# A decoder layer in fp32r pieces: when sets are summed, how far down's operands are prepared, and where the last norms stand

## The chip, the cores and the metric

The kernel runs on one core of one Trainium2 chip. A core has five engines that run their own instruction streams in order: PE (TensorE, matmuls; PEld are its weight loads), DVE (VectorE), ACT (ScalarE), POOL (GpSimd) and SP (SyncE, which only issues transfers here). ACT and POOL can issue transfers too. An instruction waits on semaphores for what it needs; whatever stands behind it on its engine waits with it. The metric is the time of one execution in microseconds (us), as the median of several runs.

## The reference: what is computed

One layer over 1024 tokens of width 1024: an adaLN modulation from a conditioning vector, a mixer of two attentions with gates, a layer norm, a SwiGLU feed-forward and a second layer norm. The change touches the last two:

```python
def swiglu(u, w_gate_up, w_down):
    h = jnp.einsum('btd,df->btf', u, w_gate_up)
    hg, hu = jnp.split(h, 2, axis=-1)
    return jnp.einsum('btf,fd->btd', jax.nn.silu(hg) * hu, w_down)
...
    y = swiglu(u, w_gate_up[l], w_down[l])
    x = layer_norm(DEEPNORM_ALPHA * x + (1.0 + gate_f) * y, ln2_g[l], ln2_b[l])
```

The feed-forward width is 2816, which is 22 tiles of 128 rows.

## The kernel before, in words

**Numbers in two pieces.** A float32 operand is split: ACT copies it, rounded, to a high piece and DVE subtracts that from the original for the low piece (`split`, lines 169 and 170; for gate/up weights lines 144 and 145). A product is then three matmuls: high by high, high by low, low by high.

**Seven products for eight.** Both feed-forward matrices are multiplied by a Strassen-like scheme: sums and differences of the four quarters of each operand give seven products of half size in place of eight. Somebody has to make these sums.

**Gate/up** (the loop from line 1597) runs over 22 pairs p of a gate and an up tile, and for each over seven slots i, one product of 12 matmuls each. The split for a product is issued before the product two places earlier, and `w_hi`/`w_lo` have four buffers, so DVE works at most some three slots ahead of TensorE. POOL makes the sums of the weights (`Pairs.add`: steps 0 to 2 in slots 2 to 4 for the next pair, step 3 in slot 3 of the pair itself) and one sum of results in slot 4 (line 1639). In slot 6 of pairs 3 to 10 it also applies the first norm's gain and bias to a row block (`gain`, lines 1372 and 1373). SP loads the raw weights of pair p+2 in slot 4 (`gu.load`, line 112) and stores the pair's h tile (line 1644).

**Sets for down** (`sum_set`, line 1520). Down needs sums of its operands: 11 sets "w" of `w_down` rows and 11 sets "h" of pairs of h tiles. A set loads two tiles as four halves on ACT's queue, waits five calls, makes two operations on DVE, in the next call two more, and two calls later stores four halves on SP's queue (line 1545). `sums_ahead` is called once in each slot, and in down once per unit, and steps up to three lanes, each with its own buffers, from pairs 4, 8 and 11 on; only lane 1 may begin a set in down. An h set may begin as soon as its second tile's pair is over.

**Down** has seven products in the order 0, 1, 2, 3, 5, 4, 6, each of 11 units u. A unit is one raw pair of tiles of 128x512 (`dn_load`, two SP transfers of 256 KB, four raw buffers), one split of 128x1024 on ACT and DVE into one of 14 operand places (`dn_prepare`: 8 in the pool `bigu`, 6 in `low`), and 12 matmuls: 3 for each of four banks t. Unit u's step first issues the splits up to unit u + 11, with loads four units beyond. After a product, four `dn_add` (lines 1671 and 1672: gate times PSUM, added to the row block) and, where a row half is final, `half_stats` (line 1268) stand on DVE. Products five and seven go on in banks that the products before them in those banks have filled and `dn_add` has read: the fifth in those of the fourth, the seventh in those of the sixth.

**The second norm.** `norm_shared` (line 1290) makes a row block's moments (DVE, with one square root on ACT), normalizes it on ACT (line 1296), and returns `finish`: times gain on DVE (line 1299), plus bias on POOL (line 1300), out on SP. In the sixth product steps j = 1, 3, 5, 7 begin the norms of rows 0 to 3 and the steps behind them finish these. In the seventh product the bank loop is outside, so that a bank is done after 33 matmuls; its row's adds, statistics and norm follow, and the last row uses `norm_quick` (lines 1283 and 1286).

Everything is under a manual schedule: an engine's order is the order of the calls.

Of the kernel before, what the change touches and what calls it, by code (L numbers as in the profile page):

```python
# [11 lines left out]
F32R = mybir.dt.float32r  # L12
I32 = mybir.dt.int32
AF = mybir.ActivationFunctionType
OP = mybir.AluOpType
# [3 lines left out]
P = 128  # L19
# [130 lines left out]
def decoder_layer(ctx: ExitStack, tc: tile.TileContext, I, out, dbg=None):  # L150
# [1139 lines left out]
    def norm_shared(tb, gb, dst):  # L1290

        z = zrow(tb)
        mv, rs = moments(tb)
        nc.vector.reciprocal(rs[:, 0:1], rs[:, 0:1])
        nc.vector.scalar_tensor_tensor(rs[:, 1:2], mv[:, 0:1], -1.0, rs[:, 0:1], op0=OP.mult, op1=OP.mult)
        nc.scalar.activation(z, z, AF.Identity, bias=rs[:, 1:2], scale=rs[:, 0:1])

        def finish():
            nc.vector.tensor_tensor(z, z, gb[:, 0], op=OP.mult)  # L1299
            nc.gpsimd.tensor_tensor(z, z, gb[:, 1], op=OP.add)  # L1300
            nc.sync.dma_start(dst[tb * P:(tb + 1) * P], z)

        return finish
# [214 lines left out]
    sets = [(kind, j) for kind in "wh" for j in range(NP)]  # L1518

    def sum_set(kind, j, x, y):  # L1520
        for i, halves in enumerate((x, y)):
            f = 2 * j + i
            src = I["w_down"][f * P:(f + 1) * P, :] if kind == "w" else h_d[f]
            for t in range(2):
                nc.scalar.dma_start(halves[t], src[:, t * TH:(t + 1) * TH])
        for _ in range(5):
            yield
        (x0, x1), (y0, y1) = x, y
        tt = nc.vector.tensor_tensor
        if kind == "w":  # L1530
            tt(x0, x1, x0, op=OP.subtract)
            tt(x1, y1, x1, op=OP.subtract)
            yield
            tt(y1, y1, x0, op=OP.subtract)
            tt(y0, y0, y1, op=OP.subtract)
        else:
            tt(y1, x1, y1, op=OP.add)
            tt(x1, x0, x1, op=OP.subtract)
            yield
            tt(x0, y1, x0, op=OP.subtract)  # L1540
            tt(y0, y0, x0, op=OP.subtract)
        yield
        yield
        for i, tile in enumerate((x0, x1, y0, y1)):
            nc.sync.dma_start((wt2_d if kind == "w" else hs_d)[j, i], tile)
        for _ in range(4):
            yield

    lanes = [None] * 3

    def lane_tiles(lane):
        if lane == 0:
# [8 lines left out]
        return [[x[:, H0], x[:, H1]] for x in tiles]  # L1561

    def sums_ahead(p, i):
        for lane, first in enumerate((4, 8, 11)):
            if lanes[lane] and next(lanes[lane], "end") == "end":
                lanes[lane] = None
            if (not lanes[lane] and (p, i) > (first, 0) and p < (20, NF + 1, 20)[lane] and sets
                    and (sets[0][0] == "w" or 2 * sets[0][1] + 1 < p)):
                lanes[lane] = sum_set(*sets.pop(0), *lane_tiles(lane))
                next(lanes[lane])  # L1570

# [3 lines left out]
    def dn_load(upto):  # L1575
        while len(dn_raw) < min(upto, DN):
# [8 lines left out]
            nc.sync.dma_start(raw[:, 1], {0: I["w_down"][rows, H0], 1: I["w_down"][rows, H0], 2: wt2_d[j, 3], 3: wt2_d[j, 0],  # L1585
                                          4: wt2_d[j, 1], 5: I["w_down"][rows, H1], 6: wt2_d[j, 2]}[i])

    def dn_prepare(upto, ahead):
        while len(dn_op) < min(upto, DN):
            u = len(dn_op)  # L1590
            dn_load(u + 1)
            dn_op[u] = pools["bigu" if u % 14 < 8 else "low"].tile([P, 2, 2, TH], F32R, name="dn", tag="big")
            split(dn_op[u][:, 0], dn_op[u][:, 1], dn_raw[u])
            dn_load(u + 1 + ahead)

    n = 0
    for p in range(NF):
# [11 lines left out]
        for i in range(7):  # L1609
# [35 lines left out]
            if (p, i) == (0, 4):  # L1645
                nc.scalar.activation(g[0], g[0], AF.Silu)
            if p + 1 < NF:
                if i == 4 and p + 2 < NF:
                    gu.load(p + 2)
                if i in (2, 3, 4) and p:  # L1650
                    gu.add(p + 1, i - 2)
# [22 lines left out]
    def dn_mac(ps, u, t, first, last):  # L1674
        op, c = dn_op[u], slice(t * P, (t + 1) * P)
        for n, (x, y) in enumerate(((0, 0), (0, 1), (1, 0))):
            nc.tensor.matmul(ps, op[:, x, 0, c], op[:, y, 1], start=first and n == 0, stop=last and n == 2,  # L1677
                             skip_group_check=True)

    st8 = gx.tile([P, TH], F32, name="s3", bufs=1)  # L1680
# [4 lines left out]
    for n, i in enumerate(ORDER[:-1]):  # L1685
        if i in (1, 3):
            bank = [(ps_f, ps_x)[t // 2].tile([P, TH], F32, name=("pf", "px")[t // 2]) for t in range(4)]
        ps = bank if i % 2 else bank_a
        for j in range(NP):
            u = n * NP + j  # L1690
            dn_prepare(u + 12, 4)
            for t in range(4):
                dn_mac(ps[t], u, t, i in (0, 1, 3) and j == 0, j == NP - 1)
            sums_ahead(NF, 1)
            if i == 4:
                if 1 <= j < 9 and j % 2:
                    ends.append(norm_shared(j // 2, gb2, out))
                elif 1 <= j < 9:
                    ends.pop(0)()
        tb0, eh, first = {0: (0, 0, True), 1: (0, 0, False), 2: (0, 1, True), 3: (4, 1, True), 4: (4, 1, False),  # L1700
                          5: (0, 1, False)}[i]
        for t in range(4):
            dn_add(tb0 + t, eh, ps[t], first)
            if not first:
                half_stats(tb0 + t, eh)
    dn_prepare(DN, 4)
    for t in range(4):
        for j in range(NP):
            dn_mac(bank_a[t], 6 * NP + j, t, False, j == NP - 1)
        dn_add(4 + t, 0, bank_a[t], True)  # L1710
        half_stats(4 + t, 0)
        while ends:
            ends.pop(0)()
        if t == 3:
            norm_quick(7, gb2, out)
        else:
# [78 lines left out]
```

## Time and profile before

| what | value |
|---|---|
| median of 3 runs | 1812.08 us (1809.89 to 1812.53) |
| the profiled execution's own time | 1811.52 us |
| its span, first to last instruction | 1809.7 us |
| mean granted TensorE clock | 0.993 |
| busy: PE, DVE, ACT, POOL | 1766.1, 1218.5, 844.0, 570.1 us |
| gate/up pairs 4 to 21 | about 1209 to 1572 us |
| down | about 1572 to 1798 us |

How to read it: a row of a timeline gives start and duration in us, engine, line of the kernel, operation, tile written <- tiles read, and in brackets how long the engine had been idle and what ended that. A row of waits gives who waited for whom, the total, the times and the longest. In a window, each engine has its busy time and in brackets its count of instructions. PE's matmuls overlap in the records, so that their pitch, not their duration, tells their cost. `dn` stands for the down raws and operands alike, `zt` for the row blocks, `pf` and `px` for PSUM banks, `wt_d` in a down load for the w sets.

### The profile page before, as it was taken

Reading aid. Unit: us, or ns where it says so; the run is one execution under the profiler, and the core shown is the slowest. Engines: PE = TensorE matmul, PEld = TensorE weight load, DVE = VectorE, ACT = ScalarE, POOL = GpSimd, SP = SyncE. Lnnn points to the kernel's source line nnn. Section 1 sums busy time; section 2 is a strip of 40 time slices with the busy share of each in tenths; the row PEclk is TensorE's granted clock in tenths of the full one; section 3 lists DMA queues with packets and bytes.
Section 4 is the critical chain, followed back from the end, with each engine's and each line's share of the span. In section 5 each row is a group of like instructions: output and inputs, shape, how many; then the busy total and the mean of one; then the engine's idle time right before and its main releaser. Section 6 shows DMA issues by size and latency. Waiting matters only on the chain.

```text
span 1809.7 us, 24697 instructions
## 1 busy us (share of the span) xinstructions
PE 1766.1 (98%) x8774; PEld 1446.2 (80%) x8774; DVE 1218.5 (67%) x2094; ACT 844.0 (47%) x1731; POOL 570.1 (32%) x357
## 2 busy tenths in 40 slices
PE   9999999999999999999999999999999999999977
PEld 7888888888888888888888888887777778888865
DVE  7655566566656766568648855778786775668576
ACT  6544544444445677765542225743333333444431
POOL 0232233233233332135205734166663333200021
PEclk9999999999999999999999999999999999999998
DMA  9222333333332332266577341155457675596731
GB/s 361 85 71 82 99 84 93 101 84 105 89 83 82 90 94 71 83 233 241 178 232 249 135 151 54 60 189 183 174 188 266 233 279 199 175 316 226 231 121 58
DMA packets 131099, 277.29 MB, mean 153 GB/s; under 512 B 19296, under 2 KB 29088, under 8 KB 130976
## 3 DMA queue, kind: packets, MB, share of 16 engines
q1 hardware_dynamic: 116544, 246.80, 41.2%
q10 hardware_dynamic: 13968, 27.33, 4.4%
q8 instruction: 69, 1.13, 0.3%
q0 software_dynamic: 464, 1.58, 0.2%
q14 instruction: 54, 0.44, 0.1%
HBM read 203.99 MB, written 58.03 MB: 145 GB/s over the span
## 4 chain that ended last, share of the span: by engine, by line
PE 85%; DVE 8%; issue 3%; ACT 2%; DMA 1%; POOL 1%; ACTq 0%; DVEq 0%; SPq 0%; POOLq 0%
PE pf L1037 16%; PE pj L191 9%; PE pj L193 9%; PE pj L192 9%; PE pf L1677 7%; PE p L1037 6%; PE s L623 4%; PE p L191 3%; PE p L193 3%; PE p L192 3%; PE po L684 3%; PE pt L661 3%; PE px L1677 2%; DVE w_lo L145 1%; PE pf L191 1%
## 5 line engine op out<-in xcount | busy, mean ns | idle before, releaser
L191 PE MATMUL pj<-u,w_hi 128*128 128x512 f32 x736 | 302.5, 411 | 0.0
L193 PE MATMUL pj<-u,w_lo 128*128 128x512 f32 x736 | 288.7, 392 | 0.0
L192 PE MATMUL pj<-u,w_hi 128*128 128x512 f32 x736 | 288.1, 391 | 0.0
L550 POOL TENSOR_TENSOR rb<-rb,sin_t 128x512 f32<-128x512 f32 x64 | 85.6, 1338 | 518.6 <-DVE rb L548 449.3
L145 DVE TENSOR_TENSOR w_lo<-r,w_hi 128x512 fp32r<-128x512 f32 x128 | 135.2, 1065 | 85.9 <-ACT w_hi L144 82.1
L1677 PE MATMUL pf<-dn 128*128 128x512 f32 x726 | 172.3, 392 | 13.4 <-DVE g L1671 13.4
L79 DVE TENSOR_TENSOR w_lo<-w_raw,w_hi 128x512 fp32r<-128x512 f32 x132 | 124.2, 944 | 81.4 <-ACT w_hi L78 80.8
L1677 PEld LDWEIGHTS pf<-dn 128*128 128x128 f32 x726 | 137.6, 190 | 42.6 <-issue 13.8
L191 PEld LDWEIGHTS pj<-u,w_hi 128*128 128x128 f32 x736 | 138.5, 188 | 31.7 <-issue 5.8
L193 PEld LDWEIGHTS pj<-u,w_lo 128*128 128x128 f32 x736 | 138.2, 188 | 30.8
L639 ACT ACTIVATE probs<-probs,st 128x128 f32<-128x128 f32 (+1 forms) x320 | 145.6, 461 | 30.9 <-DVE st L628 30.5
L192 PEld LDWEIGHTS pj<-u,w_hi 128*128 128x128 f32 x736 | 138.7, 188 | 22.4
L170 DVE TENSOR_TENSOR dn<-dn 128x1024 fp32r<-128x1024 f32 x77 | 94.9, 1251 | 50.5 <-ACT dn L169 49.6
L78 ACT ACTIVATE w_hi<-w_raw 128x512 fp32r<-128x512 f32 x132 | 81.8, 622 | 92.3 <-PE p L192 55.0
L169 ACT ACTIVATE dn<-dn 128x1024 fp32r<-128x1024 f32 x77 | 80.7, 1058 | 81.5 <-DMA dn<-wt_d 30.7
L551 POOL TENSOR_TENSOR r<-ra,rb 128x512 f32<-128x512 f32 x63 | 116.2, 1845 | 4.9
L663 ACT ACTIVATE ptsb<-pt 128x512 f32<-128x512 f32 (+1 forms) x128 | 63.5, 548 | 101.4 <-PE pt L661 101.1
L144 ACT ACTIVATE w_hi<-r 128x512 fp32r<-128x512 f32 x128 | 79.5, 623 | 32.4 <-DMA h_d<-g 6.3
L1300 POOL TENSOR_TENSOR zt<-zt,gb 128x1024 f32<-128x1024 f32 x7 | 20.3, 2895 | 214.6 <-DVE zt L1299 214.6
L564 ACT ACTIVATE qs<-r 64x1024 fp32r<-64x1024 f32 x38 | 40.2, 1058 | 100.7 <-POOL r L551 100.2
L565 DVE TENSOR_TENSOR qs<-r,qs 64x1024 fp32r<-64x1024 f32 x38 | 46.4, 1220 | 57.2 <-ACT qs L564 56.5
L126 POOL TENSOR_TENSOR s<-r 128x512 f32<-128x512 f32 x27 | 36.5, 1353 | 152.8 <-DVE w_lo L145 115.0
(417 smaller groups left out, 4362.8 us busy)
## 6 DMA issues: line engine op xcount, KB each, us to landing
w_raw<-in_w_in SPq DMA_DIRECT2D x100, 256.0 KB
r<-in_w_gate_up SPq DMA_DIRECT2D x44, 512.0 KB
a_raw<-in_w_ada SPq DMA_DIRECT2D x24, 512.0 KB
dn<-hs_d SPq DMA_DIRECT2D x44, 256.0 KB
dn<-wt_d SPq DMA_DIRECT2D x44, 256.0 KB
h_d<-g SPq DMA_DIRECT2D x39, 256.0 KB
dn<-h_d SPq DMA_DIRECT2D x33, 256.0 KB
dn<-in_w_down SPq DMA_DIRECT2D x33, 256.0 KB
```

Source lines behind the costliest of these rows:

```text
L78: self.nc.scalar.activation(hi, raw, AF.Copy)
L79: self.nc.vector.tensor_tensor(lo, raw, hi, op=OP.subtract)
L145: self.nc.vector.tensor_tensor(lo, src, hi, op=OP.subtract)
L170: nc.vector.tensor_tensor(lo, src, hi, op=OP.subtract)
L191: nc.tensor.matmul(ps, w[0], m[0], start=first, stop=False)
L192: nc.tensor.matmul(ps, w[0], m[1], start=False, stop=False)
L193: nc.tensor.matmul(ps, w[1], m[0], start=False, stop=last)
L550: eng.tensor_tensor(b, b, sin_t[:, s], op=OP.mult)
L551: eng.tensor_tensor(residue_half(res, r, t), by_residue(a, r), by_residue(b, r), op=OP.add)
L639: nc.scalar.activation(pr, pr, AF.Exp, scale=-1.0, bias=st[:, 0, h, b:b + 1], accum_out=st[:, 1, h, b:b + 1])
L1037: nc.tensor.matmul(ps, w[:, c], m[:, k], start=first and k == 0 and n == 0, stop=k == 3 and n == 2, skip_group_check=True)
L1677: nc.tensor.matmul(ps, op[:, x, 0, c], op[:, y, 1], start=first and n == 0, stop=last and n == 2, skip_group_check=True)
```

## The change

- `finish` adds the bias on DVE, not on POOL.
- A set's two pairs of DVE operations each wait for a granted slot: slots 0, 1, 5 and 6 of a pair, and every unit in down; a slot is granted to one lane only. A set stays in its lane one call longer after its stores. An h set that would begin in slots 0 to 2 waits for slot 3 where its tile belongs to the pair just before. The last h set is loaded on POOL's queue.
- `gu.load(p + 2)` is issued in slot 5, not 4.
- Down has 16 operand places, and 17 from unit 33 on: the weights' `w_hi`/`w_lo` buffers make two (such a unit is split in two halves), the `a_raw`/`a_lo` buffers one. Unit u's step issues splits up to unit u + 11 for u below 3, u + 13 up to 21 and u + 14 from 22 on; behind each product's last step the splits are brought up to 14 units beyond its end, ahead of its adds.
- The sixth product runs its last three units bank by bank, and the adds and statistics of a bank follow its matmuls.
- The norms of rows 0 and 1 begin in steps 3 and 5 of the sixth product; those of rows 2 and 3 in the seventh, at unit 5 of banks 0 and 1. There a bank's pending `finish` calls come ahead of its adds.

```diff
@@ norm_shared
         def finish():
             nc.vector.tensor_tensor(z, z, gb[:, 0], op=OP.mult)
-            nc.gpsimd.tensor_tensor(z, z, gb[:, 1], op=OP.add)
+            nc.vector.tensor_tensor(z, z, gb[:, 1], op=OP.add)
@@ sum_set
+        queue = nc.gpsimd if (kind, j) == ("h", NP - 1) else nc.scalar
...
-                nc.scalar.dma_start(halves[t], src[:, t * TH:(t + 1) * TH])
+                queue.dma_start(halves[t], src[:, t * TH:(t + 1) * TH])
         for _ in range(5):
             yield
...
+        while not granted():
+            yield
         if kind == "w":
             tt(x0, x1, x0, op=OP.subtract)
             tt(x1, y1, x1, op=OP.subtract)
             yield
+            while not granted():
+                yield
...
-        for _ in range(4):
+        for _ in range(5):
             yield
...
+    lanes, slot = [None] * 3, [False]
+
+    def granted():
+        free, slot[0] = slot[0], False
+        return free
@@ sums_ahead
+        slot[0] = p == NF or i in (0, 1, 5, 6)
...
-                    and (sets[0][0] == "w" or 2 * sets[0][1] + 1 < p)):
+                    and (sets[0][0] == "w" or 2 * sets[0][1] + 1 < p - (p < NF and i < 3))):
@@
+    places = ["bigu"] * 8 + ["low"] * 6 + ["w"] * 2
+
+    def dn_place(u):
+        if u == 33:
+            places.insert(0, "a")
+        place = places.pop(0)
+        places.append(place)
+        if place == "w":
+            hi, lo = [[wpool.tile([P, 512], F32R, name=s, tag=s, bufs=4) for _ in range(2)] for s in ("w_hi", "w_lo")]
+            for i in range(2):
+                split(hi[i], lo[i], dn_raw[u][:, i])
+            return hi, lo
+        if place == "a":
+            hl = [ev.tile([P, 2, TH], F32R, name=n, tag=n, bufs=1) for n in ("a_raw", "a_lo")]
+        else:
+            op = pools[place].tile([P, 2, 2, TH], F32R, name="dn", tag="big")
+            hl = [op[:, x] for x in range(2)]
+        split(*hl, dn_raw[u])
+        return [[x[:, i] for i in range(2)] for x in hl]
...
-            dn_op[u] = pools["bigu" if u % 14 < 8 else "low"].tile([P, 2, 2, TH], F32R, name="dn", tag="big")
-            split(dn_op[u][:, 0], dn_op[u][:, 1], dn_raw[u])
+            dn_op[u] = dn_place(u)
@@ gate/up loop
-                if i == 4 and p + 2 < NF:
+                if i == 5 and p + 2 < NF:
                     gu.load(p + 2)
@@ down
-        for j in range(NP):
+        shared = NP - 3 if i == 4 else NP
+        for j in range(shared):
             u = n * NP + j
-            dn_prepare(u + 12, 4)
+            dn_prepare(u + (12 if u < 3 else 14 if u < 22 else 15), 4)
...
-            if i == 4:
-                if 1 <= j < 9 and j % 2:
-                    ends.append(norm_shared(j // 2, gb2, out))
-                elif 1 <= j < 9:
-                    ends.pop(0)()
+            if i == 4 and j in (3, 5):
+                ends.append(norm_shared(j // 2 - 1, gb2, out))
+            elif ends:
+                ends.pop(0)()
+        dn_prepare(n * NP + NP + 14, 4)
         for t in range(4):
+            for j in range(shared, NP):
+                dn_mac(ps[t], n * NP + j, t, False, j == NP - 1)
             dn_add(tb0 + t, eh, ps[t], first)
             if not first:
                 half_stats(tb0 + t, eh)
-    dn_prepare(DN, 4)
     for t in range(4):
         for j in range(NP):
             dn_mac(bank_a[t], 6 * NP + j, t, False, j == NP - 1)
+            if t < 2 and j == 5:
+                ends.append(norm_shared(2 + t, gb2, out))
+        while ends:
+            ends.pop(0)()
         dn_add(4 + t, 0, bank_a[t], True)
         half_stats(4 + t, 0)
-        while ends:
-            ends.pop(0)()
```

More of the change, by code (lines that the diff above doesn't have):

```diff
@@ L1539, in sum_set @@
             yield
+            while not granted():
+                yield
             tt(x0, y1, x0, op=OP.subtract)
@@ L1545, in sum_set @@
             nc.sync.dma_start((wt2_d if kind == "w" else hs_d)[j, i], tile)
-        for _ in range(4):
+        for _ in range(5):
             yield
-    lanes = [None] * 3
+    lanes, slot = [None] * 3, [False]
+    def granted():
+        free, slot[0] = slot[0], False
+        return free
     def lane_tiles(lane):
@@ L1676, in dn_mac @@
         for n, (x, y) in enumerate(((0, 0), (0, 1), (1, 0))):
-            nc.tensor.matmul(ps, op[:, x, 0, c], op[:, y, 1], start=first and n == 0, stop=last and n == 2,
+            nc.tensor.matmul(ps, op[x][0][:, c], op[y][1], start=first and n == 0, stop=last and n == 2,
                              skip_group_check=True)
@@ L1688, in decoder_layer @@
         ps = bank if i % 2 else bank_a
-        for j in range(NP):
+        tb0, eh, first = {0: (0, 0, True), 1: (0, 0, False), 2: (0, 1, True), 3: (4, 1, True), 4: (4, 1, False),
+                          5: (0, 1, False)}[i]
+        shared = NP - 3 if i == 4 else NP
+        for j in range(shared):
             u = n * NP + j
-            dn_prepare(u + 12, 4)
+            dn_prepare(u + (12 if u < 3 else 14 if u < 22 else 15), 4)
             for t in range(4):
@@ L1694, in decoder_layer @@
             sums_ahead(NF, 1)
-            if i == 4:
-                if 1 <= j < 9 and j % 2:
-                    ends.append(norm_shared(j // 2, gb2, out))
-                elif 1 <= j < 9:
-                    ends.pop(0)()
-        tb0, eh, first = {0: (0, 0, True), 1: (0, 0, False), 2: (0, 1, True), 3: (4, 1, True), 4: (4, 1, False),
-                          5: (0, 1, False)}[i]
+            if i == 4 and j in (3, 5):
[3 more added lines that the diff above has]
+        dn_prepare(n * NP + NP + 14, 4)
         for t in range(4):
+            for j in range(shared, NP):
+                dn_mac(ps[t], n * NP + j, t, False, j == NP - 1)
             dn_add(tb0 + t, eh, ps[t], first)
```

## The prediction

> **What bounds the kernel now.** I read the page first, then the windows by stage, TensorE's waits, and the timelines at the places where TensorE stood still. The page's first row, and windows whose columns are length, then busy time and count of PE, PEld, DVE, ACT, POOL, then granted clock, DMA share, GB/s:
>
> ```profile
> PE 1766.1 (98%) x8774; PEld 1446.2 (80%) x8774; DVE 1218.5 (67%) x2094; ACT 844.0 (47%) x1731; POOL 570.1 (32%) x357
> ...
> 1209.00:1372.00 163.00, 156.32 (x679) 126.37 (x678) 124.19 (x124) 60.94 (x107) 100.88 (x56) 1.00 0.55 192
> 1372.00:1572.00 200.00, 195.02 (x841) 157.65 (x840) 136.56 (x170) 75.33 (x131) 68.92 (x47) 0.99 0.64 223
> 1753.00:1766.00 13.00, 0.00 (x0) 0.00 (x0) 10.35 (x11) 4.28 (x5) 6.51 (x2) 0.64 0.27 105
> 1766.00:1771.00 5.00, 4.79 (x13) 3.81 (x14) 4.79 (x9) 0.00 (x0) 0.00 (x0) 0.57 0.10 41
> ```
>
> TensorE sets the time, so a gain is only what it loses. Its pitch where nothing waits, and its largest wait, from the chain and the waits of the down stage:
>
> ```profile
> 1603.60 1.36 PE px L1677 x6
> ...
> ACT dn L169 <- DMA dn<-wt_d: 30.7, 23, 6.9
> PE pf L1677 <- DVE g L1671: 13.4, 1, 13.4
> ```
>
> Six matmuls in 1.36 us are 0.2267 us each. By that pitch the window 1209 to 1372 (pairs 4 to 11 of gate/up) holds 679 x 0.2267 = 153.9 us of work and loses 9.1; 1372 to 1572 (pairs 12 to 21) holds 190.6 and loses 9.4. In down one wait of 13.4 us stands out, and the 5 us behind it hold 13 matmuls, 2.9 us of work, at a granted clock of 0.57. Down loses about 13.4 + 1.9 = 15.3 there.
>
> **The end of the sixth product.** The timeline from the end of the fifth to the start of the seventh:
>
> ```profile
> 1720.92 0.69 DVE L1671 TENSOR_TENSOR g<-pf,gate 128x512 f32<-128x512 f32 x1 [3.80 <-PE pf L1677]
> ...
> 1728.51 0.69 DVE L1268 BATCH_NORM_STATS2 s<-zt 128x6 f32<-128x512 f32 x1
> 1729.12 2.34 DVE L170 TENSOR_TENSOR dn<-dn 128x1024 fp32r<-128x1024 f32 x2
> ...
> 1734.66 1.23 DVE L170 TENSOR_TENSOR dn<-dn 128x1024 fp32r<-128x1024 f32 x1 [2.26 <-ACT dn L169]
> 1735.80 1.22 DVE L1299 TENSOR_TENSOR zt<-zt,gb 128x1024 f32<-128x1024 f32 x1
> ...
> 1737.10 3.32 POOL L1300 TENSOR_TENSOR zt<-zt,gb 128x1024 f32<-128x1024 f32 x1 [167.95 <-DVE zt L1299]
> ...
> 1738.93 1.50 DVE L1295 SCALAR_TENSOR_TENSOR brs<-bmv,brs 128x1 f32<-128x1 f32 x1
> ...
> 1742.69 1.23 DVE L170 TENSOR_TENSOR dn<-dn 128x1024 fp32r<-128x1024 f32 x1 [2.26 <-ACT dn L169]
> ...
> 1765.39 0.68 DVE L1671 TENSOR_TENSOR g<-pf,gate 128x512 f32<-128x512 f32 x1
> ```
>
> DVE is the late one: adds and statistics of product five until 1729.1 (four rows at (1729.12 - 1720.92) / 4 = 2.05), then four norm cycles of 8.03 us (1734.66 to 1742.69), each for two units on which TensorE spends 5.44. Each cycle holds a 128x1 L1295 that ends only with POOL's add. The seventh product's first matmul must wait for L1671, queued behind all that.
>
> The change leaves two cycles here. POOL's 1.34 us of delay at L1295 (1.50 against 0.16 where POOL is idle) goes, a DVE add of 1.12 comes: I take 7.9 a cycle, between 8.03 and 8.03 + 1.12. On the old clock: 1729.1, four splits (units 69 to 72, at 2.34 / 2) to 1733.8, two cycles to 1749.6. TensorE ends the product at 1752.7; the first read ends at 1750.3. **The wait goes**, by a margin of 2.4, since a bank now closes 6.1 us before the product's end. TensorE gains 15.3.
>
> **The seventh product and the tail.** Rows of the last two norms:
>
> ```profile
> 1778.11 0.21 DVE L1273 BATCH_NORM_AGGREGATE bmv<-s 128x2 f32<-128x12 f32 x1
> ...
> 1779.03 0.16 DVE L1295 SCALAR_TENSOR_TENSOR brs<-bmv,brs 128x1 f32<-128x1 f32 x1
> 1779.23 1.24 ACT L1296 ACTIVATE zt<-zt,brs 128x1024 f32<-128x1024 f32 x1 [0.43 <-DVE brs L1295]
> ...
> 1798.37 0.69 DVE L1671 TENSOR_TENSOR g<-pf,gate 128x512 f32<-128x512 f32 x1 [1.72 <-PE pf L1677]
> ...
> 1800.43 1.21 DVE L1299 TENSOR_TENSOR zt<-zt,gb 128x1024 f32<-128x1024 f32 x1
> 1801.55 0.20 DVE L1273 BATCH_NORM_AGGREGATE bmv<-s 128x2 f32<-128x12 f32 x1
> 1801.72 2.34 POOL L1300 TENSOR_TENSOR zt<-zt,gb 128x1024 f32<-128x1024 f32 x1 [5.08 <-DVE zt L1299]
> ...
> 1801.86 3.27 DVE L1283 SCALAR_TENSOR_TENSOR zt<-zt,bmv,gb 128x1024 f32<-128x1024 f32 x1
> ...
> 1805.24 1.42 DVE L1286 SCALAR_TENSOR_TENSOR zt<-zt,brs,gb 128x512 f32<-128x512 f32 x2
> ```
>
> A norm is 1.12 to its Identity, 1.24 for that, and now 2 x 1.12 on DVE: 4.6. DVE's chain: product six's adds from 1749.6 to 1757.8; norm 2 to 1762.4; row 4's adds (bank ready at 1752.7 + 33 x 0.2267 = 1760.2) to 1764.5; norms 4 and 3 together, with one wait of ACT between, to 1772.0; row 5's adds to 1774.1; then 4.6 + 2.05 a row: row 6's adds end at 1780.7, row 7's begin at 1785.3. TensorE ends at 1752.7 + 132 x 0.2267 = 1782.6, so the last adds are 2.5 late against their bank. Old start 1798.4: 13.1 earlier. Behind it L1299's 1.12 has moved ahead, and L1283, no longer beside POOL's add, falls from 3.27 to 1.2 (L1299's row): 3.2. **Sum: -16.3**; bounds -18.8 (DVE not late) and -8 (one cycle more).
>
> **Fifteen ahead.** This edit has a price. In DVE's order the adds stand behind the splits prepared ahead: product four's adds stood behind unit 54 and now stand behind unit 57.
>
> ```profile
> 1687.11 1.06 ACT L169 ACTIVATE dn<-dn 128x1024 fp32r<-128x1024 f32 x1 [1.54 <-DMA dn<-wt_d]
> ...
> 1689.32 1.06 ACT L169 ACTIVATE dn<-dn 128x1024 fp32r<-128x1024 f32 x1 [1.15 <-PE px L1677]
> 1690.00 0.69 DVE L1671 TENSOR_TENSOR g<-pf,gate 128x512 f32<-128x512 f32 x1 [3.18 <-PE pf L1677]
> ...
> 1694.73 0.96 PE L1677 MATMUL px<-dn 128*128 128x512 f32 x3 [0.37 <-DVE g L1671]
> ```
>
> Unit 55's raw lands only at 1687.1, unit 57's, issued 2.6 later, near 1689.7; ACT and DVE finish it near 1692. So far the lead has been set by loads (the 30.7 us of ACT's waits), not by places. Moreover set (h,9) is now stored in down, not in pair 21: followed through the code slot by slot, one more MB while the DMA engines are full:
>
> ```profile
> 1582.00:1592.00 10.00, 10.00 (x46) 8.29 (x45) 5.72 (x5) 4.24 (x4) 0.00 (x0) 1.00 0.96 347
> ...
> 1487.00:1490.00 3.00, 3.00 (x8) 2.31 (x8) 2.75 (x5) 0.12 (x1) 0.00 (x0) 0.50 0.66 216
> ```
>
> At 347 GB/s that is 3 us, of which I take 1.5, as later slices have slack. The adds then begin near 1693.5, not 1690.0, and product five, on the same banks, starts 3.5 later. A gap of 2.0 us near 1484 was followed by a clock of 0.50 (the row above): 1.7 more, taken at 1.0. **Sum: +4.5**, bounds 0 and +8. [...]
>
> The two-tile places cost two half splits for one: hidden by DVE's waits for raws. Set (h,10) goes to POOL's queue, ahead of which nothing stands in down; its operations come five units later (10 and 11), and unit 32's loads stand behind its store by two units: nothing.
>
> **The sets.** POOL and DVE in pair 6 (two timelines), two set operations on the same tiles in pairs 12 to 21 (groups by line: count, busy, mean ns, idle before), and TensorE's largest wait there (total, times, longest):
>
> ```profile
> 1270.43 2.73 POOL L1373 TENSOR_TENSOR zt<-zt,gb 128x1024 f32<-128x1024 f32 x1
> 1270.94 2.77 DVE L1535 TENSOR_TENSOR w_raw<-w_raw,s 128x512 f32<-128x512 f32 x1
> ...
> L1541 DVE TENSOR_TENSOR gb<-gb 128x512 f32<-128x512 f32 x3 | 4.0, 1339 | 0.1
> L1538 DVE TENSOR_TENSOR gb<-gb 128x512 f32<-128x512 f32 x3 | 2.1, 692 | 0.1
> ...
> PE pf L1037 <- DVE w_lo L145: 3.4, 4, 2.0
> ```
>
> An operation on two SBUF tiles takes 0.69, or lasts until POOL's has ended: L1535 ends at 1273.71, POOL's at 1273.16. Slots 5, 6, 0, 1 free pairs 12 to 21 of crowding: one pair of operations (1.4) a slot, DVE at most 3.3 in one slot, under 10.9 in four. Slot 1 still meets POOL's first sum. Of 9.4 I leave 2. The extra yield, and h sets held until slot 3, spare ACT waits for stores. In pairs 4 to 11 the gain (L1372, L1373) occupies POOL in just slots 6 and 0, where sets now go: one more pair of operations before a split, three times 1.4, while two waits of about that size behind sets in slots 2 to 4 go; 9.1 becomes 10.5. **Sum: -6**; bounds -11 and +1. Loading raws at slot 5 puts SP's two transfers behind the last split that reads their buffers, so that the set and h stores queued behind them on SP are not held; POOL reads the new raws four slots (4 x 12 matmuls, 10.9 us) later and its sums are split five slots after that: nothing.
>
> **In all** -16.3 + 4.5 - 6 = -17.8 against the profiled run's own 1811.5 (span 1809.7): 1793.7. That run lies 0.6 under the median of 1812.1; I say **1794**, own range 1788 to 1800.
>
> **Rivals.**
> - Product four's adds are not later (loads catch up; ACT no longer stops for (h,10)): 1811.5 - 16.3 - 6 = 1789. Against it: the 1.54 wait for unit 55.
> - Gate/up gives nothing, as the sets meet gain and POOL's late sums: 1800. For it: L1535's 2.77.
> - Product six still waits: one cycle of 8 us more, -8 + 4.5 - 6: 1802.
> [...]
> - Slower: gate/up raws land too late. ACT splits them seven slots, 19 us, after the issue; from there each us is lost in each of 18 pairs, and 1 us suffices to undo everything, 2.7 give 1843. Against it: 1 MB in 19 us is 55 GB/s, the window moves 223.
>
> **How the numbers follow.** Forecast 0.54; rivals in order 0.16, 0.16, 0.05, 0.03, 0.04; 0.02 is left for no change. Range 1786 to 1803: both -6 bounds and the half-lost wait lie in it. Under 0.2% (3.6 us) can't be told from no change: faster 0.92, same 0.03, slower 0.05.
>
> **What would show it.** No wait of TensorE over 3 us in down; L1295 at 0.16 everywhere; L1283 near 1.2; DVE's last L1671 about 2.5 behind TensorE's end; product four's L1671 standing behind three more L170, with a TensorE gap of 2 to 4 us; pairs 12 to 21 losing about 2 us, 4 to 11 about 10. Wrong if the 13 us wait stands elsewhere, or if set operations still meet POOL.

## The result, and the profile after

The changed kernel takes 1800.05 us (median, 1799.01 to 1803.2) against 1811.35 us for the kernel before, run beside it: a ratio of 0.9942, 95% interval 0.9929 to 0.9955, so 0.58% faster. The profiled execution took 1799.96 us, with a span of 1798.2 and a mean granted clock of 0.996. It is 11.5 us shorter in span than the one before; 17.8 had been forecast.

First the page's row of busy times, and windows of the changed kernel (length, then busy time and count of PE, PEld, DVE, ACT, POOL, granted clock, DMA share, GB/s). Losses are read as in the prediction, length less 0.2267 us a matmul:

```profile
PE 1763.0 (98%) x8774; PEld 1445.9 (80%) x8774; DVE 1215.2 (68%) x2109; ACT 847.2 (47%) x1739; POOL 551.5 (31%) x354
...
1209.00:1372.00 163.00, 152.74 (x661) 122.70 (x660) 125.67 (x121) 59.25 (x105) 99.35 (x54) 1.00 0.50 177
1372.00:1569.00 197.00, 195.57 (x863) 161.38 (x862) 133.56 (x171) 76.98 (x134) 70.39 (x49) 1.00 0.68 234
1693.00:1699.00 6.00, 5.37 (x13) 3.75 (x14) 5.86 (x9) 2.80 (x3) 0.00 (x0) 0.52 0.50 172
```

Pairs 4 to 11 of gate/up now lose 163 - 661 x 0.2267 = 13.2 us (9.1 before), pairs 12 to 21 lose 197 - 863 x 0.2267 = 1.4 (9.4 before). The third window lies in down: 13 matmuls, 2.9 us of work, in 6 us at a clock of 0.52. What stands there, in the timeline of the end of product four:

```profile
1689.26 1.23 DVE L170 TENSOR_TENSOR dn<-dn 128x1024 fp32r<-128x1024 f32 x1 [0.48 <-ACT dn L169]
...
1691.66 1.23 DVE L170 TENSOR_TENSOR dn<-dn 128x1024 fp32r<-128x1024 f32 x1 [1.18 <-ACT dn L169]
1692.63 1.06 ACT L169 ACTIVATE dn<-dn 128x1024 fp32r<-128x1024 f32 x1 [1.00 <-DMA dn<-wt_d]
1692.80 0.69 DVE L1702 TENSOR_TENSOR g<-pf,gate 128x512 f32<-128x512 f32 x1
...
1693.63 0.76 PE L1708 MATMUL pf<-dn 128*128 128x512 f32 x1 [4.76 <-DVE g L1702]
```

TensorE waits 4.76 us for the first add of product four, which on DVE stands behind splits that come as slowly as their raws land. The end of the sixth product, by contrast, has no wait:

```profile
1752.96 0.68 DVE L1702 TENSOR_TENSOR g<-pf,gate 128x512 f32<-128x512 f32 x1
...
1756.08 0.85 PE L1708 MATMUL pf<-dn 128*128 128x512 f32 x3
```

The seventh product begins at 1756.08 with the three matmuls of its first unit in bank 0, without idle time; the read that it needs had ended at 1753.64, 2.4 earlier. And the last row block:

```profile
1785.43 0.84 PE L1708 MATMUL pf<-dn 128*128 128x512 f32 x3
...
1789.57 0.68 DVE L1702 TENSOR_TENSOR g<-pf,gate 128x512 f32<-128x512 f32 x1
...
1792.06 1.28 DVE L1283 SCALAR_TENSOR_TENSOR zt<-zt,bmv,gb 128x1024 f32<-128x1024 f32 x1
```

TensorE is done at 1786.1 (three matmuls of 0.2267 from 1785.43), DVE's last adds begin 3.5 later (0.2 in the kernel before), and L1283 takes 1.28, not 3.27.

With losses taken exactly, from the first matmul of one product to that of the next, the 11.5 us are: sixth and seventh product -15.4, gate/up and what precedes it -3.2, products four and five +6.6 (7.6 against 1.0), last adds +3.3, what follows them -2.8.

### The profile page after: what moved, and what is told of

Its sections match the earlier page's. It is cut to its first block, busy times and chain, and to the rows that moved or that the text cites. A ratio compares the mean times of both kernels' runs of the same rounds, so it can differ in the third digit from the quotient of the medians.

```text
span 1798.2 us, 24740 instructions
## 1 busy us (share of the span) xinstructions
PE 1763.0 (98%) x8774; PEld 1445.9 (80%) x8774; DVE 1215.2 (68%) x2109; ACT 847.2 (47%) x1739; POOL 551.5 (31%) x354
## 3 DMA queue, kind: packets, MB, share of 16 engines
q8 instruction: 69, 1.13, 0.3%
## 4 chain that ended last, share of the span: by engine, by line
PE 79%; DVE 11%; DMA 3%; issue 3%; ACT 3%; POOL 0%; SPq 0%; ACTq 0%; DVEq 0%
PE pf L1037 19%; PE pj L191 9%; PE pj L193 8%; PE pj L192 8%; PE p L1037 6%; PE s L623 4%; PE p L191 3%; PE p L193 3%; PE p L192 3%; PE po L684 3%; PE pt L661 3%; DVE dn L170 2%; DMA dn<-in_w_down 2%; PE pf L1708 1%; DMA dn<-wt_d 1%
## 5 line engine op out<-in xcount | busy, mean ns | idle before, releaser
L1708 PE MATMUL pf<-dn 128*128 128x512 f32 x630 | 150.5, 392 | 4.8 <-DVE g L1702 4.8
L1708 PEld LDWEIGHTS pf<-dn 128*128 128x128 f32 x630 | 118.9, 189 | 30.2 <-issue 5.2
L170 DVE TENSOR_TENSOR dn<-dn 128x1024 fp32r<-128x1024 f32 x66 | 79.4, 1223 | 44.3 <-ACT dn L169 43.2
L169 ACT ACTIVATE dn<-dn 128x1024 fp32r<-128x1024 f32 x66 | 69.6, 1061 | 78.0 <-DMA dn<-in_w_down 26.4
L623 PE MATMUL s<-kh,qs 128*128 128x256 f32 (+1 forms) x320 | 79.9, 283 | 1.9 <-DVE st L628 1.6
L623 PE MATMUL s<-kl,qs 128*128 128x256 f32 (+1 forms) x320 | 80.0, 279 | 0.0
```

Source lines behind the costliest of these rows:

```text
L170: nc.vector.tensor_tensor(lo, src, hi, op=OP.subtract)
L623: nc.tensor.matmul(pss[h][:, i, lo:], box["q"][h][:, b * P:(b + 1) * P], ks[h][:, (b - 1 + lo) * P:(b + 1) * P], start=i == 0 and n == 0, ...
L1708: nc.tensor.matmul(ps, op[x][0][:, c], op[y][1], start=first and n == 0, stop=last and n == 2, skip_group_check=True)
```

## The experiments

The table has every kernel that was run. Losses are TensorE's, in its profiled execution: in pairs 4 to 11, in pairs 12 to 21, and in products four and five together; "late" is how long after TensorE's end the last adds begin.

| kernel | median us | ratio to before, 95% | 4-11 | 12-21 | 4+5 | late |
|---|---|---|---|---|---|---|
| before | 1811.35 | 1 | 10.4 | 9.7 | 1.0 | 0.2 |
| changed | 1800.05 | .9929-.9955 | 14.6 | 1.9 | 7.6 | 3.5 |
| p4_adds_first | 1796.93 | .9904-.9931 | 16.2 | 1.9 | 3.4 | 3.4 |
| h9_early | 1796.86 | .9906-.9933 | 16.2 | 1.8 | 3.1 | 3.4 |
| pairs_open | 1800.04 | .9924-.9951 | 12.2 | 1.8 | 9.9 | 3.4 |
| quick_rows | 1797.57 | .9910-.9937 | 14.6 | 1.9 | 7.7 | 0.2 |
| both_and_quick | 1789.42 | .9869-.9896 | 14.6 | 1.8 | 1.1 | 0.2 |
| sets_ungated | 1795.90 | .9905-.9932 | 12.2 | 2.1 | 5.5 | 3.4 |
| pool_bias | 1803.65 | .9948-.9973 | 14.5 | 1.9 | 8.0 | 5.0 |
| four_norms | 1804.13 | .9949-.9976 | 14.6 | 1.8 | 11.2 | 0.2 |
| raws_slot4 | 1800.81 | .9931-.9956 | 14.6 | 1.9 | 7.9 | 3.4 |
| later_load_only | 1800.36 | .9930-.9955 | 10.4 | 9.1 | 7.8 | 3.4 |
| open_order_quick | 1789.42 | .9865-.9895 | 13.6 | 1.8 | 1.1 | 0.2 |
| step_only | 1794.79 | .9904-.9931 | 12.3 | 2.0 | 4.1 | 3.4 |

These losses go by the exact boundaries of the pairs and so stand up to 1.5 us above those of the fixed windows. How far chance goes can be read from kernels that are the same up to the end of the fifth product: `changed`, `quick_rows`, `pool_bias` and `four_norms` lose 7.6 to 11.2 us at products four and five, one execution each. In time, the changed kernel's executions lie between 1799.0 and 1803.2; all those of `p4_adds_first`, `h9_early`, `quick_rows`, `sets_ungated` and `step_only` lie below 1799.0.

### The wait at product four: order or lag

`p4_adds_first` puts the adds of product four back behind unit 54:

```diff
-            dn_prepare(u + (12 if u < 3 else 14 if u < 22 else 15), 4)
+            dn_prepare(55 if n == 3 and u >= 40 else u + (12 if u < 3 else 14 if u < 22 else 15), 4)
...
-        dn_prepare(n * NP + NP + 14, 4)
+        dn_prepare(55 if n == 3 else n * NP + NP + 14, 4)
```

> The changed kernel, but in the fourth product of down the splits are held at unit 54 until its adds are issued (units 55 to 57 follow them, in the fifth product). Theory A (the adds stand behind splits that the loads can't yet feed): the 4.8 us wait of TensorE between the fourth and fifth product falls to under 1 us and the half clock behind it (2.7 us) goes; the time falls by 5.5 to 7 us, to about 1794. Rival B (the wait comes from the loads alone, three us behind, whatever the order of the adds): the wait stays over 3 us and the time falls by less than 2.

`h9_early` exempts set (h,9) from the grants and lets it begin as in the kernel before, so that its stores are issued at 1558.0, 12 us ahead of down's first matmul; in the changed kernel they come 22 us behind it:

```diff
+        free = (kind, j) == ("h", 9)
-        while not granted():
+        while not (free or granted()):
...
-  2 * sets[0][1] + 1 < p - (p < NF and i < 3)
+  2 * sets[0][1] + 1 < p - (p < NF and i < 3 and sets[0][1] != 9)
```

> The changed kernel, but set (h,9) begins as early as before and doesn't wait for granted slots, so that its stores (1 MB) are issued in pair 21 and not in down. If the raws of down lag by 3 us because of that MB (unit 54's raw is issued 111.1 us after down's first matmul, 108.1 before the change): the lag falls to under 1 us, the wait between the fourth and fifth product from 4.8 to about 2 us, the time by 2 to 4 us, to about 1797. If the lag has another cause (the order of the adds, half splits), wait and time stay within 1 us.

Each removed a little more than half of the 7.6 us (3.4 and 3.1 are left) and about 3 us of time; in both profiled executions pair 7 lost 1.7 us more than in the changed kernel, to a stretch of half clock (1280 to 1283 us stand at 0.69 and 0.61, in the changed kernel at 1.00; see the last section). `p4_adds_first` thus misses its 5.5 to 7 us, and `h9_early` meets its 2 to 4. In the timeline of `p4_adds_first` the adds follow unit 54's split, and that split is itself late:

```profile
1688.34 1.23 DVE L170 TENSOR_TENSOR dn<-dn 128x1024 fp32r<-128x1024 f32 x1 [0.44 <-ACT dn L169]
...
1689.97 1.23 DVE L170 TENSOR_TENSOR dn<-dn 128x1024 fp32r<-128x1024 f32 x1 [0.40 <-ACT dn L169]
...
1691.11 0.68 DVE L1702 TENSOR_TENSOR g<-pf,gate 128x512 f32<-128x512 f32 x1
...
1691.94 0.47 PE L1708 MATMUL pf<-dn 128*128 128x512 f32 x1 [1.15 <-DVE g L1702]
```

The two theories had each claimed the whole; they are two parts. In `h9_early` the issue of unit 54's raw, counted from down's start, came at 106.4 us, against 111.1 in the changed kernel (111.6 to 114.3 in the three others that are the same up to there): the lag of which I had taken 1.5 us is 4.7. Whether the set's megabyte of transfers or its operations on DVE in down make it, these runs don't separate. Nor is the late set all of it: in `later_load_only` (below) (h,9) is stored ahead of down too, at 1556.6, yet unit 54's raw comes at 110.3 and 7.8 us are lost. What makes the lag there stays open.

`both_and_quick` has the two edits together, and the next one too:

```diff
-        if t == 3:
-            norm_quick(7, gb2, out)
-        else:
-            ends.append(norm_shared(4 + t, gb2, out))
+        norm_quick(4 + t, gb2, out)
```

> Edit: three edits together. Product four's adds stand behind unit 54 again, set (h,9) is freed from the grants and so stored before down starts, and all four norms of the seventh product run at once after their row. Theory (order and lag are two separate parts of the wait between the fourth and the fifth product, 5.0 + 2.6 us in the changed kernel, and each edit takes one part): the two steps lose 2 us or less together, product four's adds start near 1687 to 1689, last adds under 0.5 us late; 1790 to 1793. Rival (both edits cure the same 4 us, and a late unit 54 stays): 3 us or more are still lost there; 1794 to 1796.

```profile
1685.83 0.69 DVE L1703 TENSOR_TENSOR g<-pf,gate 128x512 f32<-128x512 f32 x1 [1.13 <-PE pf L1709]
...
1776.78 1.98 PE L1709 MATMUL pf<-dn 128*128 128x512 f32 x8
1778.79 0.69 DVE L1703 TENSOR_TENSOR g<-pf,gate 128x512 f32<-128x512 f32 x1
```

In this timeline DVE stands idle for 1.13 us and waits for TensorE, not the other way round (the adds' line is L1703 here): 1.1 us are lost in products four and five, near what the kernel before lost there (1.0), and the adds of the last row begin 0.2 after TensorE's end. 1789.42 us is under the range expected, since the wait went entirely and its stretch of half clock with it (the clock from 1685 to 1696 us is 1.00, in the changed kernel 0.69 from 1688 to 1699).

### The tail

`quick_rows` is that last edit alone: in the seventh product every row's norm is done at once on DVE, without ACT's Identity between.

> The changed kernel, but rows 4 to 6 of the last norm are normalized like row 7, in two passes of DVE with no pass of ACT between. Theory (DVE's chain of 6.7 us a row, with 1.3 us of waiting for ACT in each, makes the last adds 3.3 us late): the last row's adds begin within 0.5 us of its bank, and the time falls by 2.5 to 3.5 us, to about 1797. Rival (the end is set by output transfers on SP's queue, which ends 3.3 us after DVE's last instruction): the time falls by less than 1.

```profile
1784.63 1.75 PE L1708 MATMUL pf<-dn 128*128 128x512 f32 x7
...
1786.41 0.69 DVE L1702 TENSOR_TENSOR g<-pf,gate 128x512 f32<-128x512 f32 x1
```

TensorE ends at 1786.2 (seven matmuls from 1784.63); the adds are 0.2 late, and 2.5 us of the median and 3.3 of the span are gone. That DVE's norms in the seventh product set the end is shown.

`pool_bias` undoes the move of the bias alone:

```diff
-            nc.vector.tensor_tensor(z, z, gb[:, 1], op=OP.add)
+            nc.gpsimd.tensor_tensor(z, z, gb[:, 1], op=OP.add)
```

> Edit: only the add of beta in the norms goes back to POOL. Theory (POOL's add stretches the 128x1 operation behind it and L1283 at the end, DVE saves 1.1 a norm): the 128x1 operation takes about 1.5 and L1283 about 3.3 again, the seventh product's first matmul still doesn't wait, the last adds stay 2 to 4 us late; tail +2.1, time 1801 to 1803. Rival (moving the add only loaded DVE): last adds no more than 1.5 late, time 1797 to 1799.

```profile
1743.32 3.31 POOL L1300 TENSOR_TENSOR zt<-zt,gb 128x1024 f32<-128x1024 f32 x1 [142.88 <-DVE zt L1299]
1745.14 1.50 DVE L1295 SCALAR_TENSOR_TENSOR brs<-bmv,brs 128x1 f32<-128x1 f32 x1
...
1791.63 0.68 DVE L1702 TENSOR_TENSOR g<-pf,gate 128x512 f32<-128x512 f32 x1
1791.79 2.34 POOL L1300 TENSOR_TENSOR zt<-zt,gb 128x1024 f32<-128x1024 f32 x1 [5.01 <-DVE zt L1299]
1792.35 2.33 DVE L1703 SCALAR_TENSOR_TENSOR zt<-zt,g 128x512 f32<-128x512 f32 x1
...
1795.76 1.27 DVE L1283 SCALAR_TENSOR_TENSOR zt<-zt,bmv,gb 128x1024 f32<-128x1024 f32 x1
```

It costs 3.6 us, 0.65 more than the range expected. As expected L1295 takes 1.50 again and the seventh product doesn't wait; but the operation stretched beside POOL's add at the end is now L1703 (2.33 where it takes 0.69), and L1283 is free (1.27). The adds come 1.5 later, and 1.6 more follows behind them.

### The sixth product's norms

`four_norms` puts the two moved norms back into the sixth product:

```diff
-            if i == 4 and j in (3, 5):
-                ends.append(norm_shared(j // 2 - 1, gb2, out))
+            if i == 4 and j in (1, 3, 5, 7):
+                ends.append(norm_shared(j // 2, gb2, out))
...
-            if t < 2 and j == 5:
-                ends.append(norm_shared(2 + t, gb2, out))
```

> Edit: only the two norms that had been moved to the seventh product are put back into the sixth (four there, after j = 1, 3, 5, 7); its ends by banks and the fifteen units ahead stay. Theory (DVE's norm cycles of 8 us for two units are what made the wait): the adds of the sixth product start 14 to 16 us later, near 1768, TensorE waits 9 to 12 us at the seventh product and goes on at half clock, the last adds are on time; 1808 to 1812. Rival (with ends by banks, and with all splits three units further ahead, DVE has the room): the wait is under 3 us; 1796 to 1801.

```profile
1727.50 0.69 DVE L1702 TENSOR_TENSOR g<-pf,gate 128x512 f32<-128x512 f32 x1 [3.80 <-PE pf L1708]
...
1762.72 0.16 DVE L1295 SCALAR_TENSOR_TENSOR brs<-bmv,brs 128x1 f32<-128x1 f32 x1
1762.80 0.68 DVE L1702 TENSOR_TENSOR g<-pf,gate 128x512 f32<-128x512 f32 x1
...
1763.63 0.76 PE L1708 MATMUL pf<-dn 128*128 128x512 f32 x1 [4.21 <-DVE g L1702]
```

A wait is back, of 4.2 us and not 9 to 12, with 1.7 us lost to half clock behind it (its first matmul takes 0.76; in the changed kernel the first behind a wait took 0.76 at a clock of 0.50, and 0.50 at 1.00); the last adds are on time. From the first adds of product five to those of product six DVE takes 1762.80 - 1727.50 = 35.3 us here and 28.6 in the changed kernel, so two norms cost 6.7 us. I had charged them 8 us each, a whole cycle. But the splits in a cycle are done in any case, and of the fourth norm only the head, up to L1295, stands ahead of the adds. In the kernel before the same stretch took 1765.39 - 1720.92 = 44.5, and there the rest of the fourth cycle stood ahead of the adds too:

```profile
1758.69 1.22 DVE L170 TENSOR_TENSOR dn<-dn 128x1024 fp32r<-128x1024 f32 x1 [2.25 <-ACT dn L169]
...
1760.96 4.50 DVE L170 TENSOR_TENSOR dn<-dn 128x1024 fp32r<-128x1024 f32 x2
1765.39 0.68 DVE L1671 TENSOR_TENSOR g<-pf,gate 128x512 f32<-128x512 f32 x1
```

A wait of 2.25 for ACT, L1299, and three splits, the last of them held beside POOL's add of 3.25 us (4.50 for the two in place of 2.34), make 9.0 us between the fourth L1295 and the adds, where `four_norms` has none. So of the 15.9 us by which the sixth product's adds came forward, 6.7 belong to the norms; the other 9.2 come with the edits that `four_norms` keeps. Two of these can take the rest of the fourth cycle away: the splits that are done further ahead (eight in this stretch for eleven), and the last three units by banks, with which the step that used to finish the fourth norm comes behind the adds. Their shares were not tried by themselves. The median, 1804.13, lies between the two expectations. The profiled execution is 5.9 us longer in span than the changed kernel's, and the 3.6 of them that it loses at products four and five cannot come from the edit, since all that stands ahead of them is the same.

### The sets in gate/up

`pairs_open` grants every slot in pairs below 12:

```diff
-        slot[0] = p == NF or i in (0, 1, 5, 6)
+        slot[0] = p == NF or p < 12 or i in (0, 1, 5, 6)
```

> The changed kernel, but in pairs below 12 every slot may be granted (still one lane a slot). Theory: the grants push the sets of pairs 4 to 11 into the slots in which gain and POOL's first sum run; TensorE's loss in the window of these pairs falls from 13.3 us to about 9, as before the change, and the time by 3 to 5 us, to about 1796. Rival: the loss comes from raw weights loaded a slot later or from gain alone: no change within 1 us.

Gate/up lost 2.4 us less, and the time stayed: products four and five lost 9.9. Down's start 2 us earlier did not bring its loads forward: unit 54's raw was issued at 1680.0, and at 1680.1 in the changed kernel. Whether the one is the reason of the other is not shown, since 9.9 lies within what the same code loses there by chance (7.6 to 11.2). `sets_ungated` takes the grants away altogether:

```diff
-        free, slot[0] = slot[0], False
-        return free
+        return True
```

> Edit: the sets' operations may go in any slot (always granted); the later load of the raws, the extra step behind a set's store and down's edits stay. Theory (the grants took the 7.8 us out of pairs 12 to 21 and put part of the 4.2 into pairs 4 to 11): pairs 12 to 21 lose 8 to 10 instead of 1.9, pairs 4 to 11 lose 10 to 12 instead of 14.6; set (h,9) is stored in gate/up, so the fourth-to-fifth wait falls from 7.6 to about 3. In all 0 to +2: 1800 to 1802. Rival A (the later load relieved pairs 12 to 21): they stay below 4, and the time falls to 1793 to 1796. Rival B (what gate/up loses or gains, down gives back, through the loads): gate/up +4 and more, time within 1 of 1800 with the fourth-to-fifth wait not near 3.

My theory fell. Pairs 12 to 21 stay at 2.1, pairs 4 to 11 come to 12.2, and the time falls to 1795.90: 2.0 us come from gate/up and 2.1 from products four and five, where (h,9) is now stored 3 us behind down's start in place of 22. Rival A, the later load of the raws, was tested from both sides: `raws_slot4` undoes it alone, `later_load_only` keeps it alone.

```diff
@@ raws_slot4
-                if i == 5 and p + 2 < NF:
+                if i == 4 and p + 2 < NF:
@@ later_load_only, with sets_ungated's edit
-        for _ in range(5):
+        for _ in range(4):
             yield
...
-                    and (sets[0][0] == "w" or 2 * sets[0][1] + 1 < p - (p < NF and i < 3))):
+                    and (sets[0][0] == "w" or 2 * sets[0][1] + 1 < p)):
```

> Edit: the raws of the pair after next are loaded in slot 4 again, not in slot 5; all else as in the changed kernel, the grants too. Theory after the run without grants (it was the later load, not the grants, that took 7.8 us out of pairs 12 to 21): these lose 6 to 10 again, ScalarE waits there for transfers of h and of sets (in the kernel before 11 us in all), 1803 to 1807, or less if down gives part back. Rival (the step added behind a set's store, or the later start of h sets, did it): they still lose under 4; 1798 to 1801.

> Edit: of the edits to gate/up only the load in slot 5 stays; no grants, four steps behind a set's store, h sets begun as in the kernel before; down as in the changed kernel. Theory (the later load does it all): pairs 12 to 21 lose under 3, pairs 4 to 11 lose 11 to 13, time as without grants, 1794 to 1798. Rival (step and start of the h sets do it): pairs 12 to 21 lose 6 or more, 1799 to 1804.

That fell too. With the raws in slot 4 again nothing changes, and with the later load alone gate/up is what it was before the change. Two things differ between `later_load_only` and `sets_ungated`: the step behind a set's store, and the start of the h sets. `step_only` keeps the first and drops the second:

```diff
@@ with sets_ungated's edit
-                    and (sets[0][0] == "w" or 2 * sets[0][1] + 1 < p - (p < NF and i < 3))):
+                    and (sets[0][0] == "w" or 2 * sets[0][1] + 1 < p)):
```

> Edit: no grants, and h sets begun as in the kernel before; the step added behind a set's store and the later load stay, and down as in the changed kernel. It differs by that one step from the run with the later load alone, and by the later start of the h sets from the run without grants. Theory (the step changes the period at which the three lanes come round, so that two sets no longer fall into one slot): pairs 12 to 21 lose under 4, and 1795 to 1798. Rival (the later start of the h sets does it): they lose 7 to 10 with a wait of 2 us and more in pairs 13 to 17; 1799 to 1803.

Windows over pairs 4 to 11 and 12 to 21, of `later_load_only` and then of `step_only`, and between them what the one step removes, from the timeline of `later_load_only` in pair 17:

```profile
1209.00:1372.00 163.00, 156.43 (x679) 126.44 (x678) 124.25 (x124) 61.44 (x108) 100.27 (x56) 1.00 0.56 194
1372.00:1571.00 199.00, 194.13 (x839) 157.72 (x838) 135.51 (x170) 75.17 (x130) 69.86 (x49) 0.99 0.65 222
```

```profile
1480.46 1.47 DVE L1547 TENSOR_TENSOR gb<-gb 128x512 f32<-128x512 f32 x1
...
1481.96 1.66 DVE L1548 TENSOR_TENSOR gb<-gb 128x512 f32<-128x512 f32 x1
...
1483.54 2.35 DVE L145 TENSOR_TENSOR w_lo<-r,w_hi 128x512 fp32r<-128x512 f32 x2
1485.34 0.19 PEld L1037 LDWEIGHTS pf<-t3h,w_lo 128*128 128x128 f32 x1 [2.41 <-DVE w_lo L145]
1485.34 0.50 PE L1037 MATMUL pf<-t3h,w_lo 128*128 128x512 f32 x1 [1.99 <-DVE w_lo L145]
```

```profile
1209.00:1372.00 163.00, 154.47 (x670) 124.74 (x669) 122.61 (x121) 59.87 (x105) 100.74 (x57) 1.00 0.52 180
...
1372.00:1569.00 197.00, 195.95 (x862) 161.16 (x861) 139.53 (x173) 77.45 (x134) 69.94 (x50) 1.00 0.70 239
```

With the later load alone pairs 12 to 21 lose 199 - 839 x 0.2267 = 8.8; with the step added 197 - 862 x 0.2267 = 1.6. One step in a set's life did it, beside the later load, which both have. It has a price in pairs 4 to 11, 12.3 in place of 10.4. Without it, pair 17 has twelve set operations of three lanes in its slots 1 to 4; the two of slot 3 are stretched beside POOL's sums to 1.47 and 1.66, and the splits behind them are 2 us late. With it, pair 17 has four, in slots 3 to 5, and no slot of pairs 12 to 21 loses over 1.1 us. Number alone isn't the reason: pair 12 has eleven there and loses nothing. The step changes the period at which a lane returns; that this is how it parts the lanes is read from the order of the operations, not shown by a run of its own. Of the 5.6 us between the two medians this is only a part: in the profiled executions `step_only` begins down 3.8 us earlier and loses 3.7 less at products four and five.

So beside the step the grants earned nothing. They put set operations ahead of POOL's sums in pairs 9, 11 and 13, and cost 2.4 us in pairs 4 to 11 (14.6 against 12.2) and the lag of (h,9) in down; without them the kernel is 4 us faster. What the grants would do without the step was not run.

`open_order_quick` joins this to the down edits: no grants, the order of `p4_adds_first`, and `quick_rows`.

> Edit: no grants, product four's adds behind unit 54 as before the change, all four norms of the seventh product at once after their row. If the causes add up (gate/up 2.1 shorter without grants, 0.1 + 1.1 us lost between products four and five instead of 2.9 + 2.6, last adds on time): 1786 to 1788.5. Rival (time gained in gate/up is given back in down, as when only pairs 4 to 11 were opened): 1789 to 1791, with 2 us or more lost at product four.

At 1789.42 us it has the time of the rival and the products of the theory: no wait at product four, 1.1 us lost there. It equals `both_and_quick`, and both begin down at 1567.9 us, because of the 2.4 us that gate/up gains without grants 1.7 went to half clock behind pair 7's wait, in this execution and not in the other (below), and it came to pair 4 0.9 later. Both beat the changed kernel by 0.6% and the kernel before by 1.2%.

## Why the prediction was right or wrong, by its own steps

**The time.** 1800.05 lies in the range of 1786 to 1803, 0.05 above the forecast's own 1788 to 1800. Of 17.8 us, 6.3 did not come: 2.8 in gate/up, 2.1 at product four, 1.4 at the end. The value of the rival in which gate/up gives nothing (1800) was met, but that is not what happened: gate/up gave 3.2 us.

**The end of the sixth product: right.** The wait went, with the margin of 2.4 that was forecast; the loss there fell by 15.4 for 15.3. The sum holds term by term: in the changed kernel four adds with their statistics took 8.2 us as before, four splits 4.5 for 4.7, two cycles 15.9 for 15.8. (A cycle measured 7.96; the 7.9 taken was right, though it lies outside the 8.03 to 9.15 named for it.) What the prediction doesn't say, and `four_norms` shows, is that only 6.7 us of this belong to the two norms moved; 9.2 come with the other edits.

**The tail: right in kind, 1.4 short.** Last adds 3.5 late for 2.5 (its own clock, 1785.3 less 1782.6, gives 2.7), L1283 at 1.28 for 1.2, L1295 at 0.16 again. The DVE chain of norms and adds was the right one, as `quick_rows` shows; I had it about one microsecond short over four rows.

**Fifteen ahead: right mechanism, two terms too small.** The forecast was 3.5 us of later adds and 1.0 of half clock, and the kernel shows adds 6.0 later on down's clock, a wait of 4.8 and 2.6 of half clock, in which the three small waits of the kernel before (1.0) vanish: 7.6 - 1.0 = 6.6 for 4.5. The step that failed first is "of which I take 1.5": undone alone, the late set moved unit 54's raw by 4.7 us. That it does so by its megabyte of transfers is not shown. The half clock followed: it lasted 6.8 us behind this wait, 3.4 behind that of 2.0 on which the 1.0 was based.

**The sets: the sum was near, the reason was wrong.** "Slots 5, 6, 0, 1 free pairs 12 to 21 of crowding" failed: the same pairs are as free with every slot granted. Of the relief of 7.8 us, 7.1 came with one more step behind the store (9.1 against 2.0, in runs that differ by it alone), which the prediction names in half a sentence as sparing ACT's waits and charges at nothing. "9.1 becomes 10.5" became 13.2: between exact boundaries the loss rose by 4.2 us, of which 2.4 come with the grants and 1.9 with the step. Slot 1 met POOL's first sum as foreseen, but 2 us had been left for all of pairs 12 to 21, and pairs 9, 11 and 13 alone lost 1.8 each in slots 3 and 4. In pair 9:

```profile
1321.64 1.30 POOL L126 TENSOR_TENSOR s<-r 128x512 f32<-128x512 f32 x1 [5.69 <-DVE w_lo L145]
...
1322.89 1.76 POOL L132 TENSOR_TENSOR r<-r,s 128x512 f32<-128x512 f32 x1
1323.53 1.67 DVE L1540 TENSOR_TENSOR a_lo<-a_lo 128x512 f32<-128x512 f32 x1
...
1325.11 2.96 DVE L145 TENSOR_TENSOR w_lo<-r,w_hi 128x512 fp32r<-128x512 f32 x3
...
1326.92 0.50 PE L1037 MATMUL pf<-t3h,w_lo 128*128 128x512 f32 x1 [1.48 <-DVE w_lo L145]
```

L1540 ends 0.5 us behind POOL's L132, three splits queue behind it, and TensorE waits.

**What was put at nothing.** Raws loaded in slot 5: nothing, either way, and the slower rival (1843) with it. Set (h,10) on POOL's queue: two rows of two transfers each, whose issue took 1.16 and 1.09 us, and its first operation on DVE, at 1613.77, came 12.1 us later on down's clock, some four and a half units for the five foreseen.

```profile
1597.50 1.16 POOL L1526 DMA_DIRECT2D a_raw<-h_d  x2 [31.54 <-DMA hs_d<-a_lo]
1598.64 1.09 POOL L1526 DMA_DIRECT2D a_lo<-h_d  x2
```

POOL waited 31.54 us for the lane's last store, with nothing of its own behind; on ACT that wait would have stood ahead of down's splits, which no run tried.

## What to carry to other kernels

When a queue of periodic side work crowds the main path, look first at how its periods fall together: one step more in a cycle did here what a whole scheme of granted slots was meant to do (9.1 us lost in pairs 12 to 21 became 2.0), and beside it the scheme only cost (2.4 us in pairs 4 to 11). Work prepared further ahead on an in-order engine also stands ahead of whatever must be read next, so a deeper lead can be paid where the main path needs that engine: here product four's adds came 6.0 us later. The price goes with the lag of the loads behind it: where unit 54's raw was issued 4.7 us earlier (`h9_early`), 3.1 us were lost in place of 7.6. A gain ahead of a stage that waits for transfers (of ten windows of 10 us in down of the changed kernel, from 1579 to 1679, five have a DMA share of 0.91 to 1.05) need not show in the time: of 2 us in gate/up, nothing did in `pairs_open` (1800.04 against 1800.05).

## What the runs showed of the hardware that was not expected

**Of equal waits of 2.0 us, some were followed by half clock and some were not.** Twelve of these kernels have the same wait in pair 7, 2.0 us long; in nine the clock from 1280 to 1283 us was 1.00, in three it was lower: 0.69 in `p4_adds_first`, 0.61 in `h9_early`, 0.51 in `open_order_quick`. Timeline rows and two windows each, of the changed kernel and then of `open_order_quick`:

```profile
1279.58 0.50 PE L1037 MATMUL pf<-t2h,w_lo 128*128 128x512 f32 x1 [2.02 <-DVE w_lo L145]
...
1275.52:1278.93 3.41, 2.04 (x9) 1.31 (x7) 3.34 (x7) 0.00 (x0) 0.00 (x0) 1.00 0.91 336
1278.93:1282.35 3.42, 2.77 (x12) 2.30 (x13) 2.20 (x4) 1.31 (x3) 2.15 (x2) 1.00 0.33 125
```

```profile
1279.49 0.80 PE L1037 MATMUL pf<-t2h,w_lo 128*128 128x512 f32 x1 [2.03 <-DVE w_lo L145]
...
1276.11:1279.52 3.41, 1.38 (x7) 0.80 (x6) 3.34 (x7) 0.00 (x0) 0.00 (x0) 1.00 1.03 380
1279.52:1282.93 3.41, 3.41 (x8) 2.74 (x9) 2.19 (x3) 1.15 (x2) 2.73 (x3) 0.50 0.14 50
```

One hundredth of a microsecond apart in length, 1.00 against 0.50, and 1.7 us of time. The windows are not chosen freely. In the kernel before, half clock lasted 3.41 us from 1486.99 and 13.65 us from 1756.65; in the changed kernel, ahead of the end, 6.83 us from 1691.94. These are one, four and two times 3.413 us, and the two starts in the kernel before, 269.65 us apart, are 79 times that. The windows of `open_order_quick` end and begin where its clock changes, at 1279.52; those of the changed kernel are counted back from 1691.94 in 121 such steps, an estimate for a place where its clock does not change. In `open_order_quick` the wait lies in the one window ahead of the half clock, which so has 2.03 us without a matmul; in the kernel before the 2.03 us from 1483.98 likewise lie in the 3.41 us ahead of its half clock at 1486.99. In the changed kernel the border at 1278.93 cuts the wait into 1.37 and 0.65, and the clock stays at 1.00. In these executions of the two kernels no other wait in gate/up or down is longer than 1.75 us, save the 13.4 us of the kernel before and the 4.8 us of the changed one, which had half clock within them and behind them (0.50); the wait of 1.75, at 1272.6 in the kernel before, was followed by 1.00. That the place of such a wait among these steps decides is read from these three executions; no run moved a wait to try it.

**POOL's add stretched a different DVE operation in each order of the calls.** At the end of the kernel before it was L1283 (3.27, and 1.28 in the changed kernel, where POOL has no such add), in `pool_bias` L1703 (2.33 for 0.69), and in the fourth norm of the kernel before a split (4.50 for two in place of 2.34), while the same add of 128x1024 took POOL 2.3 to 3.3 us. Each of these ended after POOL's add had. L1273, L1275 and L1294, which read one tile each, took 0.20, 0.15 and 0.16 beside the add at 1737.10 in the kernel before; L1295 behind them, which reads two, took 1.50. So what the add cost depended here on what was queued on DVE, not on the operation that one had looked at.
